# Hymba block: the attention weights of both query pairs of a head side by side, one 256-column product at the seam

## The chip, the cores and the metric

The kernel runs on one core of a Trainium2 chip. The metric is the device time of one launch in microseconds (us); the time of a kernel is the median of its runs. A profile is one further execution, recorded by the hardware profiler; its span runs from the first to the last instruction.

The engines that matter here: TensorE (PE in the profile; its weight loads stand apart as PEld), VectorE (DVE), ScalarE (ACT), GpSimd (POOL), and SyncE (SP), whose queue issues nearly all DMAs. On-chip memory has 128 partitions; a size in KB below is always per partition.

## The reference

One decoder block over 2048 tokens of width 1024, all in float32. What matters here is the attention: 8 heads of 64 channels, queries in blocks of 128, strictly causal, with "stick-breaking" weights in place of a softmax:

```python
z = jnp.einsum('bhqd,bhkd->bhqk', qb, kb).astype(jnp.float32) * scale
mask = s_idx[None, :] < t_idx[:, None]
log1m = jnp.where(mask, jax.nn.log_sigmoid(-z), 0.0)
tail = lax.cumsum(log1m, axis=3, reverse=True) - log1m
a = jnp.where(mask, jnp.exp(jax.nn.log_sigmoid(z) + tail), 0.0)
ob = jnp.einsum('bhqk,bhkd->bhqd', a, vb.astype(jnp.float32))
```

A weight is a sigmoid times the product of all (1 - sigmoid) of the keys between it and the query. Beside the attention stand a pooling mixer, an output projection, and a feed-forward layer of width 4096 with a squared relu; each is preceded or followed by an RMS norm.

## The kernel before

**The work as a whole.** The tokens are cut into four tiles of 512 (index j). `front` runs the input projection tile pair by tile pair: a w_in chunk times the normed x gives 128 columns of pool input, q, k or v at a time, and these products are the lines 172 to 174 (one weight block each, 512 columns wide; three products per block because every float32 operand is split into a high and a low float32r part). The weight chunks come from memory through SP into `raw`, are split by ACT (L143, high part) and DVE (L144, low part) into `hl`, five granules ahead of use (`WAHEAD`). `tail` does the output projection in the same way. Then `up` (L1016) and `down` (L1251) do the feed-forward layer by a seven-product scheme (Strassen's, with P1 to P7 as names).

**The attention** is woven into the projection: after every dense step `run` calls `advance`, which takes further pieces of attention from a list. Only near keys are computed at first: each 128-query block sees its own key block and the one before it (a far part runs only if some product of (1 - sigmoid) has not reached zero; it does not run here). A unit of work, `near_unit(j, h, p, t)`, is one head h of one tile j for one **query pair** p: the two query blocks 2p and 2p+1, each with two key blocks of 128, so four pieces of 128x128. It has three stages, a generator that yields between them, and `turn_stages` (L682) moves up to three units on by one stage at a turn, the oldest first:

1. logits on PE (L611, L612, mask at L640), sigmoids on ACT, the running products on DVE (L623), the weights `sg` in the end on DVE (L649 or L653);
2. four transposes on PE (L658) into `pta`, then the split of the result into `at` (high part by ACT, low part by DVE: L660, which the profile shows as tile `at` at L143 and L144);
3. the products of the values with `at` into the PSUM tile `po` (L669), and after the second pair the sum of halves into `ot` (L628 on ACT, L629 on DVE).

The stationary operand (weights, in the sense of the array) of stage 3 is a block of values `vw[:, b]`, b being 0 for the key block before the tile and 1 to 4 for those in it; the moving operand is `at`. Within a pair the four 128-column pieces of `at` are, in order: query block 2p with key block 2p (`vw` index 2p+0), 2p with 2p+1, 2p+1 with 2p+1, 2p+1 with 2p+2. The two middle ones share their key block, so they are one product of 256 columns; the outer ones are products of 128. Each is done for the high and the low part of `at`:

```python
av = [(P, 3 * P, 1, 0), (3 * P, T, 2, P)] + ([] if c0 else [(0, P, 0, 0)])
```

That is two products of 256 and four of 128 columns for a pair; in tile j = 0 the first piece of the first pair does not exist (`c0`), so there it is two and two. The last piece of pair 0 and the first piece of pair 1 have the same key block (`vw` index 2), and are two separate products of 128 in two units.

**Memory.** Pools of tiles are stacked from the left (`const`, `vp`, then what a stage needs) and from the right. `at` is a tile of 4 KB, two buffers, one for each unit, in the pool `att` on the right. `rlast` (4 KB, the spread roots of the last two token tiles, written by ACT at L1024 and read by DVE at L917) lies in `const` at the left for the whole program. In `up` the left stack goes on with `rtp` (8 KB), `hlp` (six buffers `hw` of 4 KB), `rba` (8 KB) and so on; in `down` it is laid anew with `rlp` (16 KB), `tmp2` (19.1 KB), `rs` (three buffers `ar` of 4 KB, loaded by SP at L1073), `rt`, `t8`, `s8` and others. A tile that is laid over older ones waits for the last use of each of those it touches.

**What sets the order.** The program is written in one sequence; the framework then orders each engine's queue by priority and by a simulated timeline, and derives the waits. So a change of one piece can move its neighbours in a queue. Each engine works through its queue in order.

Of the kernel before, what the change touches and what calls it, by code (L numbers as in the profile page):

```python
# [8 lines left out]
F32 = mybir.dt.float32  # L9
F32R = mybir.dt.float32r  # L10
# [5 lines left out]
P = 128  # L16
S = 2048
D = 1024
T = 512
# [27 lines left out]
def hymba_block(ctx: ExitStack, tc: tile.TileContext, xT, gains, w_in, pool_w, w_out, w_up, w_down, out):  # L47
    nc = tc.nc
# [3 lines left out]
    const = pool("const", 1)  # L52
# [65 lines left out]
    left = [const.tile([P, TB, H], F32, name=f"left{j}") for j in range(NT)]  # L118
    zall = const.tile([P, NT], F32, name="zall")
    zeros = const.tile([1, 1], I32, name="zeros")  # L120
    rlast = const.tile([P, 2, T], F32, name="rlast")
    sslast = const.tile([P, T], F32, name="sslast")
    yrlast = const.tile([P, 2, 2, TB], F32R, name="yrlast")
    carry = const.tile([P, len(WINDOWS), PAD], F32, name="carry")
# [15 lines left out]
    def split(dst, src):  # L140

        hi, lo = dst
        nc.scalar.activation(hi, src, AF.Copy)  # L143
        return nc.vector.tensor_tensor(lo, src, hi.bitcast(F32), ALU.subtract)  # L144
# [464 lines left out]
    def logits(pz, qa, qb, b, k, first=True, last=True):  # L609
        qsl = slice(b * P, (b + 1) * P)  # L610
        nc.tensor.matmul(pz, qa[:, qsl], k, start=first, stop=False, skip_group_check=not (first and last))  # L611
        nc.tensor.matmul(pz, qb[:, qsl], k, start=False, stop=last, skip_group_check=not (first and last))  # L612

    def sigmoids(pz):
        n = pz.shape[-1]
        sh = att.tile([P, T], F32, tag="sh", name="sh")
        nc.scalar.activation(sh[:, T - n:], pz, AF.Sigmoid, scale=-0.125)
        sg = att.tile([P, T], F32, tag="sg", name="sg", bufs=3)
        nc.scalar.activation(sg[:, T - n:], pz, AF.Sigmoid, scale=0.125)
        return sh, sg  # L620

    def products_left(out_, x, first):
        nc.vector.tensor_tensor_scan(out_[:, ::-1], x[:, ::-1], x[:, ::-1], first, op0=ALU.mult, op1=ALU.bypass)  # L623

    def halves_sum(dst, po, e):

        me, other = slice(e * DH, (e + 1) * DH), slice((1 - e) * DH, (2 - e) * DH)
        nc.scalar.activation(dst[me], po[other], AF.Copy)  # L628
        nc.vector.tensor_tensor(dst[me], dst[me], po[me], ALU.add)  # L629

    def near_unit(j, h, p, t):


        c0 = P if j == 0 and p == 0 else 0
        pz = psz.tile([P, T], F32, tag="pz", name="pz")
        pc = att.tile([P, T + 4], F32, tag="pc", name="pc")
        for i in range(2):
            b, lo = 2 * p + i, c0 if i == 0 else 0
            logits(pz[:, i * 256 + lo:(i + 1) * 256], t["qa"], t["qb"], b, t["kw"][:, b * P + lo:(b + 2) * P], i == 0, False)
        nc.tensor.matmul(pz.rearrange("p (i n) -> p i n", i=2)[:, :, P:], identb, maskb, start=False, stop=True,  # L640
                         skip_group_check=True)
        sh, sg = sigmoids(pz[:, c0:])
        for i in range(2):
            r = slice(i * 256 + (c0 if i == 0 else 0), (i + 1) * 256)
            products_left(pc[:, r], sh[:, r], 1.0)

        if c0:
            for lo, hi in ((c0, 255), (256, 511)):
                nc.vector.tensor_tensor(sg[:, lo:hi], sg[:, lo:hi], pc[:, lo + 1:hi + 1], ALU.mult)  # L649
        else:  # L650
            sg2 = sg.rearrange("p (i n) -> p i n", i=2)
            pc2 = pc[:, 0:T].rearrange("p (i n) -> p i n", i=2)
            nc.vector.tensor_tensor(sg2[:, :, 0:255], sg2[:, :, 0:255], pc2[:, :, 1:256], ALU.mult)  # L653
            nc.gpsimd.tensor_copy(left[j][:, 2 * p:2 * p + 2, h], pc2[:, :, 0])
        yield
        pt = pst.tile([P, T], F32, tag="pt", name="pta")
        for x in range(c0 // P, TB):
            nc.tensor.transpose(pt[:, x * P:(x + 1) * P], sg[:, x * P:(x + 1) * P], ident)  # L658
        at = att.tile([P, 2, T], F32R, tag="at", name="at")
        split((at[:, 0, c0:], at[:, 1, c0:]), pt[:, c0:])  # L660
        yield
        if p == 0:
            t["po"] = pso.tile([P, T], F32, tag="po", name="po")
        po, vw = t["po"], t["vw"]
        av = [(P, 3 * P, 1, 0), (3 * P, T, 2, P)] + ([] if c0 else [(0, P, 0, 0)])

        for n, (lo, hi, v, to) in enumerate(av):
            for x in range(2):
                nc.tensor.matmul(po[:, p * 256 + to:p * 256 + to + hi - lo], vw[:, 2 * p + v], at[:, x, lo:hi],  # L669
                                 start=(p == 0 and n == 0 and x == 0), skip_group_check=True,  # L670
                                 stop=(p == 1 and n == len(av) - 1 and x == 1))
        if p == 1:
            if h % 2 == 0:
                t["ot"] = ots[j, h // 2] = att.tile([P, T], F32, tag="ot", name="ot", bufs=1)
            halves_sum(ots[j, h // 2], po, h % 2)
            if h % 2:
                nc.sync.dma_start(os_[j][h // 2], ots.pop((j, h // 2)))
        yield
# [9 lines left out]
    def near(j, h2):  # L688
        def load(h):
            t = {}  # L690
            t["qa"], t["qb"] = load_q(j, h)
            t["kw"] = kw = att.tile([P, P + T], F32R, tag="k", name="kw")
            t["vw"] = vw = att.tile([P, TB + 1, P], F32R, tag="vv", name="vw")
            if j > 0:
                nc.sync.dma_start(kw[:, 0:P].bitcast(F32), ks[h][j - 1][:, T - P:].bitcast(F32))
                nc.sync.dma_start(vw[:, 0].bitcast(F32), vs[h][j - 1][:, T - P:].bitcast(F32))
            nc.sync.dma_start(kw[:, P:].bitcast(F32), ks[h][j].bitcast(F32))
            nc.sync.dma_start(vw[:, 1:].rearrange("p b d -> p (b d)").bitcast(F32), vs[h][j].bitcast(F32))
            return t

        t = load(2 * h2)
        for e in range(2):
            for p in range(2):
                stages.append(near_unit(j, 2 * h2 + e, p, t))
                turn_stages()
                if p == 0:
                    t2 = load(2 * h2 + 1) if e == 0 else None
                yield 0.27
            t = t2
# [145 lines left out]
    def up(pools, more):  # L855

        saps, hlp, rba, rtp, srp = pools
        NM = NF // 2
        cols = [(q, m) for q in range(2) for m in range(NM)]

# [13 lines left out]
        def load(q, m):  # L874
            raw[q, m] = (rbb if m % 2 else rba).tile([P, 4, G, P], F32, tag="rb", name="rb")
            nc.sync.dma_start(raw[q, m], w_up[m])
# [127 lines left out]
        for g, (q, m, s) in enumerate(slots):  # L1004
# [7 lines left out]
            t, w = ps[q, m, bank], ops.pop(g)  # L1012
# [12 lines left out]
            if g + UA < len(slots):  # L1025
                make_weights(g + UA)
                q2, m2, s2 = slots[g + UA]
                n = q2 * NM + m2 + 2
                if s2 == "P3" and n < 2 * NM:
                    load(*cols[n])  # L1030
# [280 lines left out]
    def begin_ffn():  # L1311

        catch_up(len(later))
        for scope in (last_scope, out_scope, left_scope):
            scope.close()
        spool = lambda name, bufs, **kw: left_scope.enter_context(tc.tile_pool(name=name, bufs=bufs, reuse_waits="tile", **kw))
        sap = {}
        rtp, hlp, rba, srp = (spool(n, b) for n, b in (("rtp", 1), ("hlp", UA + 2), ("rba", 1), ("srp", SR)))
        for i in range(LB):
            sap[i] = spool(f"sap{i}", 2)  # L1320

        def more():
            sap[6], pup, rbb, avp = spool("sap6", 2), spool("pup", 2), spool("rbb", 1), spool("avp", 11)
            sap[4], sap[5] = (spool(f"sap{s}", 2) for s in (4, 5))
            return rbb, pup, avp, spool("psu", 2, space=PS)

        layer.append(up([sap, hlp, rba, rtp, srp], more))
        next(layer[0])
# [100 lines left out]
```

## Time and profile before

| what | value |
|---|---|
| median of 3 runs | 1945.07 us (1943.7 to 1950.17) |
| span of the profiled execution | 1941.4 us, 25998 instructions |
| mean granted clock of TensorE | 0.998 |
| attention products (L669) | x368, from 102.8 to 552.9 us |
| `up` (L1016) | from 694.5 to 1308.5 us |
| `down` (L1251) | from 1309.2 us to the end |

The profiled execution has no time of its own besides its span; the median of the runs stands 3.7 us above that span, which is what lies around the first and last instruction, and the spread of runs.

How to read the profile's lines: a group is "line engine operation out<-in", its shape, how many (x), then its busy time in us, the mean duration of one in ns, and the idle time of the engine ahead of it with what ended that. A row of the timeline is "start, duration, engine line operation out<-in", several equal ones merged with their count. The duration of a product overlaps with the next one's, since the array is a pipeline; what a product costs TensorE is the distance from its start to the next start. A window's row gives, for each engine, busy us and in brackets the count of instructions, then the granted clock, the DMA share and GB/s.

### The profile page before, as it was taken

The page shows a single profiled execution, that of the slowest core. Times are in us where ns is not written, and L with a number is a line of the kernel's source. Part 1 is how long each engine was busy: PE and PEld are TensorE (multiplying, and loading weights), DVE is VectorE, ACT ScalarE, POOL GpSimd, SP SyncE. Part 2 cuts the span into 40 slices and gives each one's busy share as a digit, 9 for nine tenths or more (in the row PEclk, how much of TensorE's full clock was granted, in tenths as well). Part 3 has the DMA queues.
Part 4 walks back from the last instruction along what each step waited for, and adds up shares of the span by engine and source line. Part 5 has one row for each costly group of instructions (what it writes and reads, how often), then busy time and mean ns, then how long its engine had stood idle before and what let it go on. Part 6 is the DMA issues. An engine that isn't in the chain of part 4 may idle for free.

```text
span 1941.4 us, 25998 instructions
## 1 busy us (share of the span) xinstructions
PE 1922.7 (99%) x9139; PEld 1605.2 (83%) x9139; DVE 1267.6 (65%) x1882; ACT 956.9 (49%) x1544; POOL 192.0 (10%) x399
## 2 busy tenths in 40 slices
PE   9999999999999999999999999999999999999997
PEld 7888888888888888888888888878888888888887
DVE  6887799668876975777586565665454443446474
ACT  5565566455544555555575555553323233424353
POOL 0211123102111110000000000000110000213010
PEclk9999999999999999999999999999999999999999
DMA  6685686888696954677564544477885554546472
GB/s 216 206 273 180 223 279 208 266 307 285 235 378 233 338 187 155 213 243 247 181 243 159 173 141 158 145 268 288 290 284 196 192 196 151 201 153 208 148 255 89
DMA packets 164845, 426.79 MB, mean 220 GB/s; under 512 B 19680, under 2 KB 25824, under 8 KB 160608
## 3 DMA queue, kind: packets, MB, share of 16 engines
q1 hardware_dynamic: 164560, 424.77, 64.1%
q8 instruction: 74, 1.21, 0.3%
q14 instruction: 67, 0.55, 0.1%
q10 hardware_dynamic: 144, 0.26, 0.0%
HBM read 284.44 MB, written 140.51 MB: 219 GB/s over the span
## 4 chain that ended last, share of the span: by engine, by line
PE 94%; DVE 3%; DMA 2%; ACT 1%; issue 0%; SPq 0%; DVEq 0%; ACTq 0%
PE pb L1251 31%; PE pY L1016 17%; PE pd L173 8%; PE pd L172 8%; PE pd L174 8%; PE pZ L1016 8%; PE pX L1016 4%; PE po L669 2%; PE pta L658 1%; PE pm L199 1%; PE pz L611 1%; PE pz L612 1%; PE pr L225 1%; DMA wr<-in_w_down_dram 1%; PE pb L1214 1%; PE pz L640 0%
## 5 line engine op out<-in xcount | busy, mean ns | idle before, releaser
L1251 PE MATMUL pb<-ad,wd 128*128 128x512 f32 x2640 | 601.6, 390 | 1.3 <-ACT ad L143 0.7
L1251 PEld LDWEIGHTS pb<-ad,wd 128*128 128x128 f32 x2640 | 494.8, 188 | 104.6 <-ACT ad L143 1.3
L1016 PE MATMUL pY<-sa,hw 128*128 128x512 f32 x1536 | 364.3, 390 | 1.2 <-ACT u L955 1.2
L1016 PEld LDWEIGHTS pY<-sa,hw 128*128 128x128 f32 x1536 | 288.1, 188 | 61.8 <-ACT u L955 2.1
L172 PE MATMUL pd<-h,hl 128*128 128x512 f32 x752 | 299.8, 399 | 0.7 <-DVE qkr L418 0.7
L173 PE MATMUL pd<-h,hl 128*128 128x512 f32 x752 | 297.2, 395 | 0.0
L174 PE MATMUL pd<-h,hl 128*128 128x512 f32 x752 | 297.0, 395 | 0.0
L143 ACT ACTIVATE ad<-ar 128x1024 fp32r<-128x1024 f32 x112 | 117.4, 1051 | 139.4 <-PE pb L1251 116.7
L1016 PE MATMUL pZ<-sa,hw 128*128 128x512 f32 x768 | 184.6, 389 | 0.0
L144 DVE TENSOR_TENSOR ad<-ar,ad 128x1024 fp32r<-128x1024 f32 x112 | 144.3, 1293 | 55.6 <-ACT ad L143 55.6
L144 DVE TENSOR_TENSOR wd<-wr,wd 128x1024 fp32r<-128x1024 f32 x64 | 82.2, 1285 | 148.9 <-ACT wd L143 148.4
L143 ACT ACTIVATE wd<-wr 128x1024 fp32r<-128x1024 f32 x64 | 67.8, 1059 | 206.0 <-PE pb L1251 198.3
L1016 PEld LDWEIGHTS pZ<-sa,hw 128*128 128x128 f32 x768 | 144.1, 188 | 29.8
L172 PEld LDWEIGHTS pd<-h,hl 128*128 128x128 f32 x752 | 142.2, 189 | 28.3 <-DVE qkr L418 1.0
L174 PEld LDWEIGHTS pd<-h,hl 128*128 128x128 f32 x752 | 141.9, 189 | 27.9
L173 PEld LDWEIGHTS pd<-h,hl 128*128 128x128 f32 x752 | 142.0, 189 | 26.8
L143 ACT ACTIVATE hl<-raw 128x512 fp32r<-128x512 f32 x168 | 104.2, 630 | 108.2 <-PE pd L174 69.9
L144 DVE TENSOR_TENSOR hl<-raw,hl 128x512 fp32r<-128x512 f32 x168 | 114.6, 687 | 51.3 <-ACT hl L143 50.9
L144 DVE TENSOR_TENSOR hw<-rt,hw 128x512 fp32r<-128x512 f32 x128 | 87.7, 688 | 76.3 <-ACT hw L143 76.1
L1016 PE MATMUL pX<-sa,hw 128*128 128x512 f32 x384 | 93.1, 389 | 0.0
L1046 DVE TENSOR_TENSOR wr<-wr 128x1024 f32<-128x1024 f32 x32 | 39.2, 1224 | 81.0 <-DMA wr<-in_w_down_dram 78.0
L955 ACT ACTIVATE u<-pY 128x512 f32<-128x512 f32 x64 | 38.1, 595 | 103.6 <-PE pY L1016 103.3
(203 smaller groups left out, 2389.7 us busy)
## 6 DMA issues: line engine op xcount, KB each, us to landing
ar<-sd SPq DMA_DIRECT2D x112, 512.0 KB, 4.5
wr<-in_w_down_dram SPq DMA_DIRECT2D x72, 512.0 KB, 3.7
rb<-in_w_up_dram SPq DMA_DIRECT2D x32, 1024.0 KB, 6.1
sd<-a SPq DMA_DIRECT2D x128, 256.0 KB, 3.7
raw<-in_w_in_dram SPq DMA_DIRECT2D x50, 512.0 KB, 4.4
sd<-s SPq DMA_DIRECT2D x96, 256.0 KB, 3.8
raw<-in_w_out_dram SPq DMA_DIRECT2D x32, 512.0 KB, 5.6
sr<-su SPq DMA_DIRECT2D x28, 512.0 KB, 5.5
```

What stands on the lines that cost most here:

```text
L143: nc.scalar.activation(hi, src, AF.Copy)
L144: return nc.vector.tensor_tensor(lo, src, hi.bitcast(F32), ALU.subtract)
L172: nc.tensor.matmul(ps, hl[:, 0, c], hi, start=(k == 0), stop=False)
L173: nc.tensor.matmul(ps, hl[:, 0, c], lo, start=False, stop=False)
L174: mm = nc.tensor.matmul(ps, hl[:, 1, c], hi, start=False, stop=(k == n - 1))
L199: marks["pm"] = nc.tensor.matmul(pm[:, c:c + 1], ss[:, c * P:(c + 1) * P], inv[n], start=(i == 0), stop=(i == len(parts) - 1))
L225: mm = nc.tensor.matmul(pr[:, b * P:(b + 1) * P], yr[:, x, b:b + 1].to_broadcast([P, P]), identr, start=(b == 0 and x == 0), stop=(b == TB ...
L669: nc.tensor.matmul(po[:, p * 256 + to:p * 256 + to + hi - lo], vw[:, 2 * p + v], at[:, x, lo:hi], start=(p == 0 and n == 0 and x == 0), sk ...
L955: nc.scalar.activation(k[name], y, AF.Copy)
L1016: nc.tensor.matmul(t, w[:, wx, c], a[:, ax, c % 2], start=first and c == 0 and x == 0, stop=last and c == G - 1 and x == 2, skip_group_che ...
L1046: nc.vector.tensor_tensor(b, a, b, ALU.subtract)
L1251: nc.tensor.matmul(ps[q, n], t[:, wx, c, n * P:(n + 1) * P], left_[q][:, ax, c], start=(n_ in ("P1", "P5", "P2") and kk == 0 and c == 0 an ...
```

## The change

`at` becomes one tile for a head, twice as wide: pair 0 writes the left 512 columns, pair 1 the right 512. Pair 0 then issues only its first piece (128 columns, not in tile 0) and its middle piece (256). Pair 1 issues the seam, which is the last piece of pair 0 and the first of pair 1 as one product of 256 columns, its own middle piece (256), and the last piece (128). For the memory that the wider `at` needs, `rlast` moves from `const` into the pool `hlp` of the feed-forward stage.

```diff
-    rlast = const.tile([P, 2, T], F32, name="rlast")
...
-        at = att.tile([P, 2, T], F32R, tag="at", name="at")
-        split((at[:, 0, c0:], at[:, 1, c0:]), pt[:, c0:])
+        if p == 0:
+            t["at"] = att.tile([P, 2, 2 * T], F32R, tag="at", name="at")
+        at, at0 = t["at"], p * T + c0
+        split((at[:, 0, at0:p * T + T], at[:, 1, at0:p * T + T]), pt[:, c0:])
         yield
...
-        av = [(P, 3 * P, 1, 0), (3 * P, T, 2, P)] + ([] if c0 else [(0, P, 0, 0)])
+        if p == 0:
+            av = ([] if c0 else [(0, P, 0, 0)]) + [(P, 3 * P, 1, 0)]
+        else:
+            av = [(3 * P, 5 * P, 2, P), (5 * P, 7 * P, 3, 2 * P), (7 * P, 8 * P, 4, 3 * P)]
...
-                nc.tensor.matmul(po[:, p * 256 + to:p * 256 + to + hi - lo], vw[:, 2 * p + v], at[:, x, lo:hi],
+                nc.tensor.matmul(po[:, to:to + hi - lo], vw[:, v], at[:, x, lo:hi],
...
     def up(pools, more):
         saps, hlp, rba, rtp, srp = pools
+        rlast = hlp.tile([P, 2, T], F32, tag="rl", name="rlast", bufs=1)
```

## The prediction

> **What bounds the kernel now.** I read the page's busy shares and its chain first, to see which engine sets the end.
>
> ```profile
> span 1941.4 us, 25998 instructions
> PE 1922.7 (99%) x9139; PEld 1605.2 (83%) x9139; DVE 1267.6 (65%) x1882; ACT 956.9 (49%) x1544; POOL 192.0 (10%) x399
> ...
> PE 94%; DVE 3%; DMA 2%; ACT 1%; issue 0%; SPq 0%; DVEq 0%; ACTq 0%
> ```
>
> PE is busy all the time, and 94% of the chain that ended last is PE. But ends of products are modelled, so a stretch that reads busy could hide waiting. The stage that the change touches is 102.8 to 552.9 us. So next come the waits of PE between 100 and 555 us, and windows of that stage.
>
> ```profile
> PE pm L199 <- DVE ss L183: 1.8, 1, 1.8
> PE pp L391 <- ACT pls L143: 0.8, 1, 0.8
> PE pp L392 <- DVE pls L144: 0.3, 1, 0.3
> ```
>
> ```profile
> 300.00:350.00 50.00, 50.00 (x289) 43.10 (x289) 47.21 (x81) 31.95 (x59) 18.04 (x30) 1.00 0.72 225
> ...
> 400.00:450.00 50.00, 48.16 (x278) 41.24 (x277) 32.63 (x55) 26.90 (x50) 2.01 (x7) 1.00 0.96 330
> ```
>
> In 455 us PE waited 2.9 us in all. So time taken off PE in this stage comes off the end, as long as nothing stands close behind. Two things do: DVE at 47.21 of 50 us (94%) around 300 to 350, and the DMA engines at 0.96 around 400 to 450.
>
> **What a product costs.** The groups by shape give the counts; their busy us are unions with neighbours, and their mean durations (261 and 299 ns) overlap, so neither is a price.
>
> ```profile
> L669 PE MATMUL po<-at,vw 128*128 128x128 f32 x240 | 34.6, 261 | 0.0
> ...
> L669 PE MATMUL po<-at,vw 128*128 128x256 f32 x128 | 32.9, 299 | 0.0
> ```
>
> The counts fit the code: 32 heads x 2 pairs x (2 wide + 4 narrow), less 2 x 8 narrow in tile 0, are 128 and 240. The price comes from start to start in the timeline of PE. First a run of one pair between dense products (the row is named after its first product; it holds 2 wide and 4 narrow), then a single wide one, then four narrow ones:
>
> ```profile
> 402.55 0.80 PE L669 MATMUL po<-at,vw 128*128 128x256 f32 x6
> 403.19 0.45 PE L173 MATMUL pd<-h,hl 128*128 128x512 f32 x1
> 403.47 0.40 PE L174 MATMUL pd<-h,hl 128*128 128x512 f32 x1
> 403.70 0.40 PE L172 MATMUL pd<-h,hl 128*128 128x512 f32 x1
> ...
> 405.32 0.28 PE L669 MATMUL po<-at,vw 128*128 128x256 f32 x1
> 405.44 0.40 PE L173 MATMUL pd<-h,hl 128*128 128x512 f32 x1
> ```
>
> ```profile
> 305.42 0.56 PE L669 MATMUL po<-at,vw 128*128 128x128 f32 x4
> 305.82 0.45 PE L172 MATMUL pd<-h,hl 128*128 128x512 f32 x1
> 306.10 0.40 PE L173 MATMUL pd<-h,hl 128*128 128x512 f32 x1
> ```
>
> A dense product of 512 columns takes 0.23 us (403.47 to 403.70). A wide one takes 405.44 - 405.32 = 0.12. After narrow ones the next dense product's start comes early but its step is longer (305.82 to 306.10 = 0.28, and 403.19 to 403.47 = 0.28, in place of 0.23), so I count to the start after that and take 0.23 off: four narrow ones are 306.10 - 305.42 - 0.23 = 0.45, or 0.1125 each. The six check it: 403.47 - 402.55 - 0.23 = 0.69, and 2 x 0.12 + 4 x 0.1125 = 0.69. **A narrow product costs nearly as much as a wide one.** By its columns it would be half. What remains the same is the load of a block of 128x128:
>
> ```profile
> L669 PEld LDWEIGHTS po<-at,vw x368: 186/189/201, 102.8 to 552.9; 128*128 128x128 f32 x184
> ```
>
> A load takes 189 ns but overlaps with its neighbours, so what sets a narrow product is most likely the load for the next one.
>
> **The change part by part.**
>
> *Products.* A head had 4 wide and 8 narrow ones (6 in tile 0). It gets 6 wide and 4 narrow (2 in tile 0). So in each of the 32 heads 4 narrow go and 2 wide come: 4 x 0.1125 - 2 x 0.12 = 0.21 us, and 32 x 0.21 = **6.7 us** off PE. In all x368 becomes x304, with 64 weight loads fewer.
>
> Here the Trainium skill speaks against the change. "TensorE: Matmul & The Clock Gate", section "Back-to-back issue gap", gives the distance of isolated products as N/2.4 + 2.5 ns: 56 ns for 128 columns, 109 for 256. By that rule the sum would be 32 x (4 x 56 - 2 x 109), 0.2 us, no gain. The trace disagrees for the narrow one (112 ns) and is near it for the wide one (120 ns); the same page's "LDWEIGHTS" section, columns/1.2, gives 107 ns for a load of 128 columns, which is near what the narrow ones show.
>
> *Seam and order.* The seam product reads what pair 0 wrote one turn earlier, so it waits for nothing new. Pair 0's last piece moves one turn later; nobody waits for it alone, since the sum of halves (L628) follows pair 1. The outer piece now goes ahead of the middle one in pair 0: same operands, price nothing.
>
> *The wide tile `at`.* Its buffer comes back after two heads, where the narrow tile's came back after two units: from one turn of slack to two. One new wait is thinkable: if the framework took the tile as a whole, pair 1's split would wait for pair 0's products, which are issued in the same turn. Rows that bear on it:
>
> ```profile
> L808 DVE TENSOR_TENSOR acc<-pd,acc x32: 679/692/703, 506.5 to 694.7; 128x512 f32<-128x512 f32 x32
> L808 DVEq EVENT_SEMAPHORE  x2: 21/36/50, 560.3 to 574.3; - x2
> its engine sat idle before it (us, times) until:
>   PE pd L174: 19.7, 15
> ```
>
> There DVE adds into one slice of `acc` while the slice before it is still being stored (L809); it sat idle for PE alone. So slices are kept apart, and I take nothing. Were it otherwise, ACT's split (and behind it in ACT's queue the weight splits `hl`) would wait for `po` products. What such a wait is worth now:
>
> ```profile
> ACT ot L628 <- PE po L669: 11.6, 6, 2.7
> ```
>
> The longest is 2.7 us, and five weight granules of 12 dense products (12 x 0.23 = 2.8 us each) lie ahead. With that cover the price is nothing; without it 32 x 2.7 = 86 us.
>
> *`rlast`.* It is written twice and read sixteen times in either place, at no other time. But `const` ends 4 KB lower, and `hlp` is 4 KB larger. In `up` everything behind `hlp` stays where it was. In `down` everything lies 4 KB lower: `rs` begins 16 + 19.1 = 35.1 KB above `const`, where `rtp` and `hlp` now reach to 8 + 28 = 36 KB instead of 32. So the first `ar` buffer now touches the last buffer `hw`, and its load must wait for that buffer's last use. With six buffers in turn and 224 slots, that is slot 221, P7 of the last column.
>
> ```profile
> 1278.90 1.27 SPq L1073 DMA_DIRECT2D ar<-sd  x3
> ...
> 1299.22 2.88 PE L1016 MATMUL pY<-sa,hw 128*128 128x512 f32 x12
> ...
> 1305.64 2.88 PE L1016 MATMUL pZ<-sa,hw 128*128 128x512 f32 x12
> ...
> 1308.13 2.94 ACT L143 ACTIVATE ad<-ar 128x1024 fp32r<-128x1024 f32 x3
> ...
> 1309.22 2.21 PE L1251 MATMUL pb<-ad,wd 128*128 128x512 f32 x8 [0.70 <-ACT ad L143]
> ```
>
> ```profile
> DMA to landing us min/median/max: 3.1/4.5/7.6
> ```
>
> The load was issued at 1278.90. It would now be issued when the twelve products from 1299.22 are done, about 1302.0; with the median of 4.5 us from issue to landing that is 1306.5, still ahead of its split at 1308.13. Behind it on SP's queue stand weight loads and stores of `up`; it can't stand ahead of any that P7 itself needs. Price between nothing and, if it were issued only when the last products of `up` end at 1308.5, 1308.5 + 4.5 - 1308.13 = 4.9 us. I take nothing, as 1306.5 is on the early side.
>
> *What is late next.* One place in the stage is set by weights and not by PE:
>
> ```profile
> 446.59 1.15 ACT L143 ACTIVATE hl<-raw 128x512 fp32r<-128x512 f32 x2 [4.72 <-DMA raw<-in_w_in_dram]
> ...
> 448.69 1.02 PE L199 MATMUL pm<-inv,ss 128*128 128x1 f32 x8 [1.84 <-DVE ss L183]
> ```
>
> ```profile
> 450.50:454.00 3.50, 3.50 (x11) 2.78 (x10) 1.57 (x4) 1.80 (x4) 0.20 (x2) 0.51 0.97 303
> ```
>
> ```profile
> 400.00:450.00 50.00, 6.62 (x48) 6.46 (x48) 2.40 (x4) 2.37 (x4) 1.00 0.96 330
> ```
>
> A weight chunk landed late while the DMA engines were full, PE ran dry for 1.84 us, and the granted clock was then 0.51 for 3.5 us: 1.84 + 0.49 x 3.5 = **3.6 us** for one such event. What PE gains shortly ahead of that wait only lengthens it. Of the 368 products 48 lie in 400 to 450 (0.9 us of the gain); I write off half, 0.4 us.
>
> **Sum:** 6.7 - 0.4 = 6.3 us. The span goes from 1941.4 to 1935.1. The median of the runs stands 3.7 us above the span, and I leave that as it is: 1945.07 - 6.3 = **1938.8 us**, or 0.32% less.
>
> **The rivals.**
>
> *Given back later.* The full price at the change from `up` to `down`, 4.9 us, leaves 1943.7. For it: that first `ar` load loses 23 us of lead. Against: it still has 1.6.
>
> *By the column.* If a product cost by its width (0.23/512 of a us per column: 57 and 114 ns), nothing is saved: 1945.1. (It is what the Trainium skill's rule above would do.) The 0.45 us for four narrow ones speaks against it.
>
> *New dry spots, slower than before.* The queues are ordered anew, and PE comes earlier to weights that DMA sets. Place: 400 to 460 us. Each further event like the one above costs 3.6 us, so from two on the gain is gone: 1938.8 + 7.2 = 1946.0. For it: share 0.96 there, and DVE at 94% around 300. Against: PE had just one such event in 455 us, and all that it gains is 6.7 us over these. The Trainium skill ("TensorE: Matmul & The Clock Gate", "What's actually happening") has the clock fall after an idle window of about 3.4 us; by that rule a 1.84 us gap would cost only itself. The trace shows 0.51 behind such a gap, so the trace's price stands.
>
> *The dry spot at 446 goes.* The same reordering could remove it: 1938.8 - 3.6 = 1935.2.
>
> **How the numbers follow.** Forecast 0.62 (1936.5 to 1941), given back 0.18, by the column 0.05, dry spots 0.10, spot gone 0.05. A difference of 0.3%, 5.8 us, is about what a measurement of this kernel can tell from no change; that is 1939.2, just above the forecast, so I put 0.42 of the forecast's 0.62 on faster and 0.20 within. With the spot gone, faster is 0.47. Within: 0.20 + 0.18 + 0.05 + half of the dry spots = 0.48. Slower by over 0.3% needs four events: 0.05. The range goes from the spot gone, with 1 us for the spread of runs, 1934, to two dry spots, 1946.
>
> **What would show it.** Right: L669 x304 (112 narrow, 192 wide), the same 0.12 and 0.11 us from start to start, PE's waits in the stage still about 3 us, and the first product of L1251 about 6.3 us earlier than 1309.22. Wrong: narrow ones that get dearer beside wide ones; a second stretch with a granted clock near 0.5 before 555; ACT waiting for `po` ahead of `at` (L143); ACT `ad` (L143) waiting for DMA `ar` at the start of `down`. The forecast fails if the new order of the queues moves more than the products save.

## The result, and the profile after

The changed kernel takes **1953.87 us** (median of 5 runs, 1950.64 to 1956.38) against 1945.07 (5 runs, 1942.02 to 1950.17): a ratio of 1.0042, 95% interval 1.0027 to 1.0056. It became slower by 8.8 us; the forecast was 6.3 us faster. The profiled execution spans 1952.0 us, 10.6 more than before. The medians are 8.8 apart and not 10.6: a run's time stands 1.8 to 1.9 us above its span in all later runs, so the 3.7 us of the kernel before also held some 1.9 us by which its profiled execution was quicker than its median.

The page of the changed kernel, first its busy time and the chain that ended last, then the two groups of the attention products:

```profile
span 1952.0 us, 25864 instructions
PE 1916.5 (98%) x9075; PEld 1598.3 (82%) x9075; DVE 1268.0 (65%) x1882; ACT 955.9 (49%) x1544; POOL 203.1 (10%) x399
...
PE 92%; DMA 3%; DVE 3%; ACT 1%; issue 0%; SPq 0%; DVEq 0%; ACTq 0%
```

```profile
L673 PE MATMUL po<-at,vw 128*128 128x256 f32 x192 | 37.9, 293 | 0.0
L673 PE MATMUL po<-at,vw 128*128 128x128 f32 x112 | 20.2, 249 | 0.0
```

The products are the ones that were forecast, 192 wide and 112 narrow, and PE is busy for 6.2 us less (1922.7 to 1916.5). Yet the span is longer, so PE must wait somewhere for some 17 us more than it did. The waits of PE over the whole span say where:

```profile
PE pb L1256 <- ACT ad L142: 11.2, 1, 11.2
PE pY L1021 <- ACT u L960: 1.8, 2, 1.1
...
PE pm L198 <- DVE ss L182: 1.6, 1, 1.6
...
PE ptv L434 <- ACT vf L431: 1.1, 1, 1.1
PE pd L171 <- ACT vf L431: 1.0, 1, 1.0
PE pd L173 <- DVE hl L143: 0.9, 1, 0.9
```

One wait of 11.2 us stands ahead of the first product of `down` (it was 0.70). Three new ones of about 1 us (those for `vf` and `hl`) stand in the attention and the output projection. The timeline from the end of `up` on, engines mixed:

```profile
1307.94 0.63 ACT L954 ACTIVATE a<-a 128x512 f32<-128x512 f32 x1 [2.69 <-DVE a L990]
1308.19 0.32 SPq L951 DMA_DIRECT2D sd<-s  x1
1308.60 0.63 ACT L955 ACTIVATE a<-a 128x512 f32<-128x512 f32 x1
...
1309.73 0.32 SPq L951 DMA_DIRECT2D sd<-a  x1
1310.38 1.62 SPq L1078 DMA_DIRECT2D ar<-sd  x3
...
1316.79 1.06 ACT L142 ACTIVATE ad<-ar 128x1024 fp32r<-128x1024 f32 x1 [7.57 <-DMA ar<-sd]
...
1317.90 0.80 PE L1256 MATMUL pb<-ad,wd 128*128 128x512 f32 x1 [11.23 <-ACT ad L142]
```

The first load of `ar`, issued at 1278.90 before, is now issued at 1310.38: SP takes it only behind all but two of the stores of the last results of `up` (`sd`), and those stores wait for ACT and DVE. It lands 6.4 us later, its split takes 1.06 us, and PE starts at 1317.90 in place of 1309.22. Windows around that (the fourth last column is POOL, then come the granted clock, the DMA share and GB/s):

```profile
1306.60:1317.90 11.30, 0.07 (x1) 0.00 (x0) 2.02 (x5) 2.31 (x3) 0.00 (x0) 0.72 1.03 404
1317.90:1322.00 4.10, 4.10 (x10) 3.29 (x11) 3.64 (x3) 2.12 (x2) 0.00 (x0) 0.53 0.65 215
1322.00:1330.00 8.00, 8.00 (x37) 6.60 (x36) 3.68 (x3) 3.18 (x3) 0.00 (x0) 1.00 0.79 237
```

The clock fell in the wait, and PE worked the next 4.1 us at 0.53: 4.1 x 0.47 = 1.9 us more. **The sum closes:** the first product of `down` comes 1317.90 - 1309.22 = 8.7 us later, and 8.7 + 1.9 = 10.6, the difference of the spans. Ahead of that point the change did gain: the last products of `up` end 1.85 us earlier than before (1303.79 + 2.88 = 1306.67 against 1305.64 + 2.88 = 1308.52), though that is far less than 6.3. Some of it is not even the change's: the first logits product already starts 1.1 us earlier (89.7 against 90.8 us), before any product that was changed.

So two things are to be explained: the wait ahead of `down`, and where 4 to 5 us of the gain went before it.

### The profile page after: what moved, and what is told of

Read it like the earlier page. It is cut to its first block, busy times and chain, and to the rows that moved or that the text cites. A ratio compares the mean times of both kernels' runs of the same rounds, so it can differ in the third digit from the quotient of the medians.

```text
span 1952.0 us, 25864 instructions
## 1 busy us (share of the span) xinstructions
PE 1916.5 (98%) x9075; PEld 1598.3 (82%) x9075; DVE 1268.0 (65%) x1882; ACT 955.9 (49%) x1544; POOL 203.1 (10%) x399
## 4 chain that ended last, share of the span: by engine, by line
PE 92%; DMA 3%; DVE 3%; ACT 1%; issue 0%; SPq 0%; DVEq 0%; ACTq 0%
PE pb L1256 31%; PE pY L1021 18%; PE pZ L1021 9%; PE pd L171 8%; PE pd L173 8%; PE pd L172 8%; PE pX L1021 4%; PE po L673 1%; PE pta L657 1%; PE pm L198 1%; DMA raw<-in_w_in_dram 1%; PE pz L610 1%; PE pz L611 1%; PE pr L224 1%; PE pb L1219 1%; DVE nt L256 1%
## 5 line engine op out<-in xcount | busy, mean ns | idle before, releaser
L1256 PE MATMUL pb<-ad,wd 128*128 128x512 f32 x2640 | 602.9, 390 | 11.2 <-ACT ad L142 11.2
```

Source lines behind the costliest of these rows:

```text
L1256: nc.tensor.matmul(ps[q, n], t[:, wx, c, n * P:(n + 1) * P], left_[q][:, ax, c], start=(n_ in ("P1", "P5", "P2") and kk == 0 and c == 0 an ...
```

## The experiments

**The wait ahead of `down`: memory or order?** Theory M: it comes from `rlast`, which lowers `const` by 4 KB and makes `hlp` 4 KB larger, so that the first `ar` buffer lies over the region of the last `hw` buffer. Rival R: it comes from the new order of the queues. The first two kernels undo the memory alone, and do the memory alone. Both leave the order of the queues nearly as it was: in the traces 4 of ACT's 1544 instructions stand elsewhere than in the kernel that each is made from.

*e1_spacer*, from the changed kernel:

```diff
-                lastv["ss"] = tmp_.tile([P, T], F32, tag="ssl", name="ssl", bufs=1)
+                lastv["ss"] = tmp_.tile([P, 3 * T], F32, tag="ssl", name="ssl", bufs=1)[:, 0:T]
```

> The changed kernel with 4 KB more in front of `rs` in `down` (the tile ssl is made three times as wide), so that every tile from there on lies where it lay before the change; attention untouched. Theory M (memory: the first `ar` buffer lies over a weight buffer `hw` of `up`, its load is queued late on SP): the 11.2 us wait of PE ahead of the first product of `down` goes back to 0.7 us, and the time falls by about 11 us from 1953.9 to 1942 to 1943, with the first `ar` load issued before 1285 us. Theory R (the new order of the attention's products upset the queues to the end): the wait stays over 8 us and the time within 3 us of 1953.9.

Measured: 1941.3 us, ratio to before 0.9982 (0.9973 to 0.9991). The wait for ACT is 0.26 us, and the first `ar` load is issued at 1277.45. Rows of SP and PE:

```profile
1277.45 1.27 SPq L1078 DMA_DIRECT2D ar<-sd  x3
```

```profile
1307.34 2.21 PE L1256 MATMUL pb<-ad,wd 128*128 128x512 f32 x8 [0.26 <-ACT ad L142]
```

*e2_rlast_only*, from the kernel before:

```diff
-    rlast = const.tile([P, 2, T], F32, name="rlast")
...
         saps, hlp, rba, rtp, srp = pools
+        rlast = hlp.tile([P, 2, T], F32, tag="rl", name="rlast", bufs=1)
```

> The kernel before, with nothing but `rlast` moved from const into hlp; `at` and the products as before. Theory M: the wait ahead of `down` appears here too, 9 to 13 us, and the time is 1954 to 1959, that is 10 to 13 us over before. Theory R: no such wait, 1943 to 1947.

Measured: 1956.4 us, ratio 1.0064 (1.0047 to 1.0081), 11.9 us over before in the medians. Rows of SP and of PE:

```profile
1311.67 1.61 SPq L1073 DMA_DIRECT2D ar<-sd  x3
```

```profile
1319.17 6.20 PE L1251 MATMUL pb<-ad,wd 128*128 128x512 f32 x20 [11.13 <-ACT ad L142]
```

The whole wait is there without any change in the attention. R is out.

*Where exactly is the edge?* Two more kernels differ from e1_spacer only in the size of the spacer. *e4_gap_1000* has `[P, T + 256]` (1.0 KB), *e5_gap_1125* has `[P, T + 288]` (1.125 KB).

> The changed kernel with a spacer of 1.0 KB in place of 4 KB: the first `ar` buffer then begins 0.03 KB above the last byte of the weight buffers `hw`, but still 0.125 KB inside the pool `hlp`, which ends with alignment padding. If the wait is tied to the region of the last `hw` buffer with its padding, it stays as in the changed kernel: 9 to 13 us ahead of `down`, time 1951 to 1956. If it were tied to the bytes of `hw` alone, or to the total shift, it would be gone: 1940 to 1943.

> The same with a spacer of 1.125 KB: the first `ar` buffer begins just where `hlp` ends, 2.9 KB lower than in the kernel before. Theory M: the wait is gone (under 1 us) and the time 1940 to 1943, though all other tiles of `down` still lie lower than before. If the shift as such mattered, it stays at 1951 to 1956.

Measured: e4 1952.2 us, 1.0038 (1.0026 to 1.0050); e5 1938.7 us, 0.9956 (0.9940 to 0.9972). PE and SP, first of e4, then of e5:

```profile
PE pb L1256 <- ACT ad L142: 10.4, 1, 10.4
```

```profile
1306.31 1.68 SPq L1078 DMA_DIRECT2D ar<-sd  x3
```

```profile
1274.66 1.27 SPq L1078 DMA_DIRECT2D ar<-sd  x3
```

```profile
1304.24 2.20 PE L1256 MATMUL pb<-ad,wd 128*128 128x512 f32 x8
```

A step of 0.125 KB moves the load by 31.7 us and the time by 13.5 (by some 10 if the larger set of runs of e12 below, the same kernel as e5, is taken). It isn't the bytes of `hw` that count (e4 is clear of them), but the end of the pool's region, padding and all; and it isn't the shift as such, for in e5 every tile of `down` from `rs` on still lies 2.9 KB lower than before.

**What is the seam worth?** *e3_wide_old_products* has e1_spacer's memory and the old products:

```diff
-        if p == 0:
-            av = ([] if c0 else [(0, P, 0, 0)]) + [(P, 3 * P, 1, 0)]
-        else:
-            av = [(3 * P, 5 * P, 2, P), (5 * P, 7 * P, 3, 2 * P), (7 * P, 8 * P, 4, 3 * P)]
+        av = [(P, 3 * P, 1, 0), (3 * P, T, 2, P)] + ([] if c0 else [(0, P, 0, 0)])
...
-                nc.tensor.matmul(po[:, to:to + hi - lo], vw[:, v], at[:, x, lo:hi],
+                nc.tensor.matmul(po[:, p * 256 + to:p * 256 + to + hi - lo], vw[:, 2 * p + v], at[:, x, p * T + lo:p * T + hi],
```

> Memory as in e1_spacer (wide `at`, `rlast` in hlp, 4 KB spacer), but each pair does its own products again: four of 128 and two of 256 columns, x368 in all; each reads its own half of the wide tile. The difference to e1_spacer is what the seam alone is worth. By the sum of the prediction it is 6.3 to 6.7 us (this kernel 1945 if e1_spacer is 1938.8). By the trace of the changed kernel, in which only about 4 us had been gained by 560 us and 2 were lost again by 680, it is 2 to 4 us: this kernel 1945, e1_spacer 1941 to 1943.

Measured: 1944.7 us, 1.0000 (0.9990 to 1.0010). So the wide tile and the place of `rlast` cost nothing that these runs can tell (2 us either way) once the edge is avoided, and the seam alone brings 1944.7 - 1941.3 = 3.4 us. That is half of its price. Either the price is wrong, or something takes half back. To tell these apart the price was made large against the rest: in *e6_seam_x4* (from e1_spacer) and *e7_old_x4* (from e3_wide_old_products) each product is issued four times.

```diff
-            for x in range(2):
+            for x, rep in ((x, rep) for x in range(2) for rep in range(4)):
```

> As e1_spacer, but every product of the values with `at` is issued four times in a row (the attention output comes out four times too large). 912 products are added. By the prices from start to start (0.111 us for 128 columns, 0.12 for 256) they cost 3 x 35.5 = 106 us: 1941.3 + 106 = 2048. What counts is the distance to e7_old_x4.

> As e3_wide_old_products, every product issued four times (attention output four times too large). 1104 products are added: 3 x 42.0 = 126 us, 1944.7 + 126 = 2071. Theory P (a seam pair is worth 0.2 us in PE time, 6.5 us for the whole, and the queues' order took half of it back): e7 minus e6 is about 4 x 6.5 = 26 us, less up to 4 for the order. Theory S (the seam itself is worth only the 3.4 us seen between e3 and e1): e7 minus e6 is about 14 us.

Measured: e6 2036.3 us, e7 2061.7 (ratios to before 1.0460, 1.0443 to 1.0478, and 1.0591, 1.0574 to 1.0609). The distance is **25.4 us**, against 26 by the price and 14 by the rival. The price holds: a quarter of it is 6.35 us. That quarter still has the first copies in it, with whatever the order took there; the three added copies alone give (117.1 - 95.0) / 3 = 7.4. The forecast's 6.7 lies between. The sums in themselves were 8 to 12% high: 95.0 us were added to e1 and 117.1 to e3, not 106 and 126.

**Who takes half back?** e1_spacer's waits of PE between 60 and 700 us, then those of e3_wide_old_products:

```profile
PE pm L198 <- DVE ss L182: 1.4, 1, 1.4
PE ptv L434 <- ACT vf L431: 1.1, 1, 1.1
PE pd L171 <- ACT vf L431: 1.1, 1, 1.1
PE pd L173 <- DVE hl L143: 0.9, 1, 0.9
PE pp L390 <- ACT pls L142: 0.8, 1, 0.8
PE pd L171 <- DVE qkr L417: 0.7, 1, 0.7
PE pp L391 <- DVE pls L143: 0.3, 1, 0.3
PE pd L171 <- DVE qk L143: 0.3, 1, 0.3
PE pr L224 <- POOL yr L234: 0.3, 1, 0.3
PE pr L224 <- POOL yr L235: 0.2, 1, 0.2
```

```profile
PE pm L198 <- DVE ss L182: 1.9, 1, 1.9
PE pp L390 <- ACT pls L142: 0.9, 1, 0.9
PE pd L171 <- DVE qkr L417: 0.7, 1, 0.7
PE pp L391 <- DVE pls L143: 0.3, 1, 0.3
```

They add up to 7.1 us against 3.8. The 3.3 us between them are of the size of what is missing (6.35 - 3.4 = 3.0). The new ones are for the most part waits for ACT and DVE, whose queues are ordered otherwise than with the old products (in the traces 108 of ACT's 1544 instructions stand elsewhere).

The account isn't closed by this, though, for the two profiles differ in the clock as well. In e3_wide_old_products it falls to 0.50 for 3.4 us behind the wait for `ss`, as in the kernel before; in e1_spacer it doesn't fall. First e3_wide_old_products, then e1_spacer:

```profile
451.50:454.90 3.40, 3.40 (x10) 2.62 (x9) 1.25 (x3) 1.91 (x4) 0.31 (x2) 0.50 1.01 345
```

```profile
451.50:454.90 3.40, 3.40 (x24) 3.08 (x23) 3.39 (x7) 2.44 (x5) 2.21 (x6) 1.00 1.03 372
```

That costs e3_wide_old_products 0.5 x 3.4 = 1.7 us. So from the first logits product to the first product of `up` the seam should lead by 6.35 - 3.3 + 1.7 = 4.7 us, and it leads by 2.7 (from 90.9 to 691.7 us against 91.5 to 695.0). Two us stay open. The timeline of e1_spacer at one of the new waits:

```profile
358.58 0.62 ACT L142 ACTIVATE mix<-nt 128x512 fp32r<-128x512 f32 x1
...
359.10 0.59 ACT L431 ACTIVATE vf<-pd 128x512 f32<-128x512 f32 x1
...
359.74 0.66 PE L434 MATMUL ptv<-ident,vf 128*128 128x128 f32 x4 [1.08 <-ACT vf L431]
```

PE needs `vf`, and ACT does a split of the norm (`mix`) first. Does the loss belong to the seam (theory S2), or to the order that the queues happened to get (theory Q)? Four kernels change one number, the pace at which attention is woven in, which reorders the queues and leaves the work as it is: `yield 0.26` and `yield 0.28` in place of `yield 0.27`, once with the seam (from e1_spacer), once with the old products (from e3_wide_old_products).

> As e1_spacer, with the pace of the attention changed from 0.27 to 0.26 (the line `yield 0.27`): the same work in another order in the queues (about 140 of 1547 ACT and 385 of 1884 DVE instructions stand elsewhere). Theory Q (what the seam lacks is lost to waits that come with the order): kernels of the same work scatter by 2 to 5 us, so this one lies anywhere from 1936 to 1945, with other waits of PE than e1_spacer. Theory S2 (the lack belongs to the seam, not to the order): 1941 plus or minus 1.

> As e1_spacer, pace 0.28. Theory Q: anywhere from 1936 to 1945, with other waits of PE. Theory S2: 1941 plus or minus 1.

> As e3_wide_old_products (products of each pair on their own), pace 0.26. Theory Q: anywhere from 1942 to 1950, and the distance to e8_seam_pace26 anywhere from 1 to 10 us with a mean near 6. Theory S2: 1944.7 plus or minus 1, and 3.4 us from e8.

> As e3_wide_old_products, pace 0.28. Theory Q: anywhere from 1942 to 1950. Theory S2: 1944.7 plus or minus 1, and 3.4 us from e9.

| pace | old products | seam | difference |
|---|---|---|---|
| 0.26 | 1947.4 us, 1.0008 (0.9998 to 1.0018) | 1939.4 us, 0.9969 (0.9957 to 0.9981) | 8.0 |
| 0.27 | 1944.7 us, 1.0000 (0.9990 to 1.0010) | 1941.3 us, 0.9982 (0.9973 to 0.9991) | 3.4 |
| 0.28 | 1950.3 us, 1.0026 (1.0014 to 1.0039) | 1944.4 us, 1.0002 (0.9989 to 1.0014) | 5.9 |

The rows 0.26 and 0.28 ran on another chip than the row 0.27; the kernel before took 1945.7 us there and 1944.5 here. So the differences within a row and the ratios hold, and times within a column compare only to about 1 us. By the ratios the same work scatters over three orders by 0.33% with the seam (6.4 us) and by 0.26% without (5.1 us). The seam is worth 3.4 to 8.0 us, 5.8 in the mean.

S2 is out: it had 1941 plus or minus 1 for both new kernels with the seam, and 3.4 us in each row. The times fit Q, except that 1950.3 lies just above its range. But what makes the scatter is shown in part only. Without the seam, the waits of PE between 60 and 700 us add up to 5.8, 3.8 and 7.2 us down the column, and the times go with them. With the seam they are 6.7, 7.1 and 7.1, and yet the times differ by 5 us; there the waits only move. In e9_seam_pace28 the largest of them is one that e1_spacer has with 0.3:

```profile
PE pr L224 <- POOL yr L234: 3.1, 2, 1.7
```

The profiled execution of e9_seam_pace28 took 1942.3 us at a granted clock of 0.998. The mean over its ten runs is 0.9959, against 0.9971 for e1_spacer's twelve: 0.0012 x 1940 = 2.3 of the 3.1 us between the two kernels. So part of the scatter lies in how often the clock falls, and no profile here shows those falls in the slower runs.

*e12_gap_1125_again* ran the kernel of e5 with more runs.

> The kernel of e5_gap_1125 again, with more runs: its queues hold the same instructions in the same order as e1_spacer's, yet its few runs gave a ratio of 0.9956 and e1_spacer's 0.9982. If both are one kernel with the spread of runs between, this gives 0.996 to 0.998; if the lower place of the tiles of `down` is worth something by itself, 0.9956 again.

Measured: 1941.2 us, 0.9986 (0.9977 to 0.9995). That is above the range that was expected and close to e1_spacer's 0.9982, so the lower place of the tiles of `down` is not shown to be worth anything. The intervals of the two measurements of this one kernel don't meet (0.9940 to 0.9972 before). The first had three runs, all with a granted clock of 0.998, on another chip; which of these made it quicker stays open. With a spacer of 1.125 KB or more the changed kernel beats the kernel before by 0.14 to 0.18% on the larger sets of runs at this pace; at pace 0.28 it does not (1.0002).

## Why the prediction was wrong, point by point

**What bounds the kernel** was right: PE's time counts at the end, as e6 and e7 show, where added products priced at 126 - 106 = 20 us apart came out 22.1 us further apart in time.

**The price of the products** was right: 6.7 us forecast, 6.35 to 7.4 measured by the fourfold kernels. The rival "by the column" is out.

**The wide tile adds no wait**: right. In the changed kernel ACT waits ahead of `at` for the transposes `pta`, and DVE for ACT's part; nobody waits there for `po`:

```profile
its engine sat idle before it (us, times) until:
  PE pta L657: 18.2, 15
  ACT at L142: 6.6, 9
  DVE at L143: 0.2, 1
```

**The `rlast` step is the one that failed.** It named the right tile, the right buffer and the right load, and then took nothing, with 4.9 us as the upper end. What was measured is 11.2 us of waiting and 1.9 us of slow clock. It came with the sign that the prediction had named for being wrong: ACT's `ad` waits for the load of `ar` at the start of `down` (7.57 us). Three things were wrong in it.

First, the place in the queue. It bounded only how early the load could stand in SP's queue, and took for the latest moment the end of the last products of `up`. But in the queue as built the load stands behind the stores of the last results but two, after its memory comes free. These stores wait for work of ACT and DVE that follows the last products: 1310.38, not 1302.0, and not even the 1306.67 at which the products ended.

Second, the landing: 6.4 us in place of the median 4.5, at a DMA share of 1.03.

Third, the clock was priced for the dry spot at 446 us, but not here, where the wait is six times as long.

Which product held the buffer last was wrong as well: the built program gives it to P5 and not to P7, so the buffers don't go in turn. This decided nothing, since the load came later than either.

**What is late next** was too small: 0.4 us written off, about 3 lost at this pace (6.35 less the 3.4 between e1 and e3); the new waits of PE are part of that, and not all of it is accounted for. The rival "new dry spots" had the right kind of cause, a new order of the queues. But the new spots were of about 1 us and for ACT and DVE, not of 3.6 us and for DMA, and without the wait ahead of `down` the kernel was not slower (e1: 0.9982).

**The rivals.** "Given back later" was the case that came about, at 0.18 and with 1943.7 us. With the price that it had in truth, 11.2 + 1.9 in place of 4.9, the time would have come out at about 1952, outside the range.

## What to carry to other kernels

When a change moves a tile to another pool, write down what lies over what in every later stage, with the padding of the pools, and take each new overlap with a live tile as a transfer that may lose its whole lead: ask what the transfer is queued behind, not only when its memory comes free. A gain in the instructions' own time and the scatter from one order of the queues to another are of the same size here (6 and 5 us), so a small change is measured by several orders of the same work, or by multiplying what it changes, and not by one build.

## What the runs showed of the hardware

The clock can stay low for longer than the wait itself. In the kernel before, a gap of 1.84 us was followed by 3.5 us at 0.51 in the window quoted in the prediction. But a gap of that size doesn't always bring a fall. At the same wait for `ss` the mean clock from 440 to 460 us is 0.91 in the four profiles with gaps of 1.6 to 1.9 us (before, changed, e2, e3) and 1.00 in the four with 0.3 to 1.5 us (e1, e4, e5, e12); elsewhere e9 has a gap of 1.7 us with the clock at 1.00 around it. So the 3.6 us that the prediction put on one such event is what it cost in that trace, and not a fixed price.

In the changed kernel the clock was low through the second half of the 11.2 us and 4.1 us beyond:

```profile
1311.50:1322.00 10.50, 4.10 (x10) 3.29 (x11) 3.65 (x3) 3.17 (x3) 0.00 (x0) 0.51 0.88 334
```

A product of 128 columns is no cheaper than one of 256 in long runs. The additions of the fourfold kernels give two equations (720 narrow and 384 wide cost 117.1 us, 336 narrow and 576 wide cost 95.0), and so 0.108 us for a narrow and 0.102 for a wide one. The kernels compared ran on two chips and in several orders of the queues, which by the table of paces is some 3 us in each sum; within that the two are the same. By the Trainium skill ("TensorE: Matmul & The Clock Gate", "LDWEIGHTS") the load of 128 columns takes 107 ns; both products stand at about that.
